# Gate rows through DRAM, an up projection with stationary tokens and transposes, and two modulation blocks per PSUM bank

## The chip, the cores and the metric

One core of a Trainium2 chip runs the whole program. The metric is the device time of one execution in microseconds (us), lower is better; 2327.01 us is the median of three runs of the kernel before.

## What is computed

One step of a transformer trunk with two layers, on 128 context tokens (`xp`) and 128 latent tokens (`xs`), width 2048, in fp32. Each layer makes six modulation vectors per stream from a conditioning vector (`w_ada`, 2048 x 12288), then an attention block and a squared-ReLU MLP of width 8192, both between RMS norms and with a gate on the residual. Cut to what matters here, for one of the two streams:

```python
sh_a, sc_a, gt_a, sh_m, sc_m, gt_m = split(silu(cvec) @ w_ada[l] + b_ada[l], 6)
h = rms_norm(x, g_pre_a) * (1 + sc_a) + sh_a
o = attention(h @ w_in[l]) @ w_out[l]
x = x + gt_a * rms_norm(o, g_post_a)
h = rms_norm(x, g_pre_m) * (1 + sc_m) + sh_m
x = x + gt_m * rms_norm(square(relu(h @ w_up[l])) @ w_down[l], g_post_m)
```

The two token streams pass through the same weights, each with its own modulation; the keys and values of the context tokens are outputs as well.

## The kernel before, in words

**Weights.** Every weight comes once from DRAM as a tile `raw` of 1 MB (128 x 2048), five in flight (`NRAW`), through SP's queue (`issue`, L994). Products are made from a high and a low half in fp32r: ACT copies half a tile to `wh` (L1011), DVE subtracts it to `wl` (L1012), and three matmuls (high x high, high x low, low x high) take the place of one. Three `wh`/`wl` pairs are in flight.

**Token-stationary groups.** The input, output and down projections use the class `Group` (L320): the tokens of stream s (`xh`, `xl`, 128 x 128) are stationary, 512 weight columns move, and a group of 1024 columns holds four accumulators, one PSUM bank each. In the last tile of a group each accumulator gets its last six matmuls together, and its `done` is called at once.

**Up projection.** The class `UpGroup` (L357) has the weights stationary (128 x 128) and the 256 tokens of both streams moving, so that the hidden units come out on the partitions, as the down projection needs them. A group is 512 hidden units in two banks; each bank gets a Relu, a square, a copy to the high half (ACT, L910, L911, L914) and a subtraction (DVE, L915). There are 16 groups in a layer; four of them and then a quarter of the down projection (2048 of 8192 rows) make one of the four rounds of the MLP.

**Modulation.** A block is 512 of a modulation vector's 2048 values, for both streams. Some blocks are made on PE (`ada_mm`, L139): 16 small matmuls from four raw tiles into one bank, a copy to `pt` (ACT, L150), four transposes, a reduction on DVE. The others are made on DVE (`dv_mul`, L195): `w_ada` transposed, multiplied by silu(c) broadcast to all partitions (`sB`), two passes (L201) for each of four tiles. The first two blocks come in halves of 256 columns. Lists of blocks are woven between the weight tiles by `weave`, and the generators in `fast`, `slow` and `dvq` are stepped once a half tile.

**Gates.** The gate of a block stays on the partitions (`gates`, L153) and is needed along the free axis. `gate_bc` (L277) transposes a broadcast column 128 x 128 four times on PE for each stream and each 512 columns: in the output projection a copy (L859) puts it in `rows`, ahead of the last tile of each half; at the end of the down projection DVE multiplies straight from PSUM (L934).

The code is recorded in this order, and a scheduler then sets the order on each engine from a model of its own; the section on the change shows places of it.

Of the kernel before, what the change touches and what calls it, by code (L numbers as in the profile page):

```python
# [67 lines left out]
def trunk(ctx: ExitStack, tc: tile.TileContext, I, O):  # L68
# [23 lines left out]
    sT = const.tile([P, KT, 32], F32, name="sT")  # L92
# [9 lines left out]
    st1 = const.tile([P, 8], F32, name="st1")  # L102
# [19 lines left out]
    def startup():  # L122
# [10 lines left out]
        for v in range(2):  # L133
            act.activation(sT[:, :, v], cT[:, v, :], AF.Silu)
# [4 lines left out]
    def ada_mm(l, sec, blk, kq, raw, half=None):  # L139

        w = 512 if half is None else 256
        if kq == 0:
            ada_live["ps"] = ps.tile([P, 512], F32, tag="ada", bufs=1, name="ada")
        pa = ada_live["ps"]
        for g in range(4):
            pe.matmul(pa[32 * g:32 * g + 32, 0:w], sT[:, 4 * kq + g, :], raw[:, g * w:(g + 1) * w],  # L146
                      start=(kq == 0), stop=(kq == 3), tile_position=(0, 32 * g))
        if kq == 3:
            pt = sb([P, 512], "pt")
            mark["pt"] = act.activation(pt[:, 0:w], pa[:, 0:w], AF.Copy)  # L150
            fast.append(ada_post(l, sec, blk, pt, 0 if half is None else 2 * half, w // P))

    gates = [const.tile([P, KT, 2], F32, name=f"gate{w}") for w in range(2)]  # L153
    made = set()

    def ada_post(l, sec, blk, pt, j0, nj):
# [5 lines left out]
        red = st1[:, 0:2 * nj].rearrange("p (j v) -> p j v", v=2)  # L162
        dve.tensor_reduce(red, m[:, 0:nj * P].rearrange("p (j g c) -> p j c g", g=4, c=32)[:, :, 0:2, :], AX.X,
                          ALU.add)
        if sec in (2, 5):
            gate_fin(l, sec, blk, red)
        else:
            mod_fin(l, sec, blk, red, j0, nj)
# [17 lines left out]
    sB = [const.tile([P, D], F32, name=f"sB{v}") for v in range(2)]  # L186
    dv_live = {}

    def load_sb():
        for v in range(2):  # L190
            nc.sync.dma_start(sB[v], I["crow"][v:v + 1, :].to_broadcast([P, D]))
        for v in range(2):
            act.activation(sB[v], sB[v], AF.Silu)

# [18 lines left out]
    def gate_fin(l, sec, blk, red):  # L213
# [3 lines left out]
        for v in range(2):  # L217
            o = gates[w][:, k0:k0 + 4, v]
            dve.tensor_tensor(o, red[:, :, v], baT[:, l, 16 * sec + k0:16 * sec + k0 + 4], ALU.add)
            dve.tensor_tensor(o, o, ngT[:, l, 2 * w + 1, k0:k0 + 4], ALU.mult)  # L220
        made.add((l, w, blk))

# [53 lines left out]

    def gate_bc(l, w, s, n):  # L277

        m = psm()
        assert (l, w, n) in made  # L280
        for j in range(4):
            tr(m[:, j * P:(j + 1) * P], gates[w][:, 4 * n + j, s:s + 1].to_broadcast([P, P]))
        return m
# [72 lines left out]

    class UpGroup:  # L357


        def __init__(self, done):  # L360
            self.done = done
            self.acc = None
            self.cnt = 0

        n = 1

# [19 lines left out]
        def left(self):  # L386
            return KT - self.cnt
# [753 lines left out]
```

## Time and profile before

| | |
|---|---|
| three runs | 2328.2, 2325.15, 2327.01 us; median 2327.01 |
| the profiled execution | 2328.18 us, its span 2326.2 us |
| PE busy | 2256.3 us, 97% of the span |
| DVE busy | 1596.9 us, 69% |
| ACT busy | 1091.7 us, 47% |
| DMA | 601.22 MB, 258 GB/s over the span |
| granted TensorE clock | 0.991 |

The span runs from the first to the last instruction of the program; the 2 us that remain lie around it. Busy times of engines overlap. The input and output projections of layer 0 take the time to about 480 us, its MLP to 1211 us; layer 1 follows, with its MLP from 1588 to 2313 us. PE stands for matmuls, and a matmul's row shows a modelled end, so the distance between two starts is the better measure of its cost in a dense stretch.

### The profile page before, as it was taken

To read this page: it belongs to the slowest core of one execution; us is meant where nothing else is said; L and a number is where in the kernel's file an instruction comes from. 1 tells how busy PE (TensorE), PEld (TensorE's weight loads), DVE (VectorE), ACT (ScalarE), POOL (GpSimd) and SP (SyncE) were. 2 spreads that over 40 slices of the span, in tenths; PEclk is the share of its full clock that TensorE was granted. 3 is DMA by queue.
4 is the path that set the end of the run, shared out by engine and by line. 5 is a ranking of instruction groups with operands and counts; after the bars stand their busy time and mean duration, and the time that the engine had idled before them with its cause. 6 is when DMAs were issued, how large, how long until landed. Compare 5 with 4: busy or idle time off the path is not lost.

```text
span 2326.2 us, 32947 instructions
## 1 busy us (share of the span) xinstructions
PE 2256.3 (97%) x13448; PEld 1905.2 (82%) x13448; DVE 1596.9 (69%) x1980; ACT 1091.7 (47%) x1508; POOL 24.6 (1%) x30
## 2 busy tenths in 40 slices
PE   6999999989999999999999999998999999999997
PEld 3567666679899889889877877877989989988986
DVE  2566745388988998998758787547566566565445
ACT  4334445365444445435446455546544444443543
POOL 0000000000000000000000000000000000000000
PEclk9999999999999999999999999999999999999999
DMA  8888787877877777787856666665566566666552
GB/s 336 302 337 338 285 314 292 345 275 283 312 296 293 279 289 292 275 304 287 344 195 258 245 248 223 227 235 201 216 235 224 204 225 219 215 219 216 182 181 91
DMA packets 92352, 601.22 MB, mean 258 GB/s; under 512 B 13736, under 2 KB 16040, under 8 KB 21288
## 3 DMA queue, kind: packets, MB, share of 16 engines
q1 hardware_dynamic: 91624, 598.64, 69.6%
q8 instruction: 105, 1.72, 0.3%
q10 hardware_dynamic: 576, 0.48, 0.1%
q14 instruction: 47, 0.39, 0.0%
HBM read 591.48 MB, written 7.60 MB: 258 GB/s over the span
## 4 chain that ended last, share of the span: by engine, by line
PE 84%; DVE 8%; DMA 4%; issue 2%; ACT 2%; POOL 1%; POOLq 0%; DVEq 0%; SPq 0%; ACTq 0%
PE acc L345 16%; PE acc L344 16%; PE acc L346 16%; PE acc L381 10%; PE acc L380 10%; PE acc L379 10%; PE ada L146 3%; DVE wl L1012 3%; PE m L120 2%; DMA raw<-w_adaT_in 2%; DVE raw L201 1%; POOL st L107 1%; PE m L467 1%; DVE stg L305 1%; ACT wh L1011 0%
## 5 line engine op out<-in xcount | busy, mean ns | idle before, releaser
L1011 ACT ACTIVATE wh<-raw 128x1024 fp32r<-128x1024 f32 x720 | 758.8, 1059 | 903.9 <-PE acc L346 527.8
L1012 DVE TENSOR_TENSOR wl<-raw,wh 128x1024 fp32r<-128x1024 f32 x720 | 874.2, 1222 | 429.6 <-ACT wh L1011 428.3
L379 PE MATMUL acc<-XT,wh 128*128 128x256 f32 x2048 | 580.1, 284 | 2.5 <-ACT XT L258 2.5
L381 PE MATMUL acc<-XT,wl 128*128 128x256 f32 x2048 | 580.7, 284 | 1.0 <-DVE wl L1012 1.0
L380 PE MATMUL acc<-XT,wh 128*128 128x256 f32 x2048 | 580.4, 284 | 0.3 <-DVE XT L259 0.3
L344 PE MATMUL acc<-wh,big 128*128 128x512 f32 x1280 | 501.9, 394 | 0.0
L345 PE MATMUL acc<-wl,big 128*128 128x512 f32 x1280 | 500.1, 391 | 1.7 <-DVE wl L1012 1.6
L346 PE MATMUL acc<-wh,big 128*128 128x512 f32 x1280 | 497.9, 390 | 0.0
L379 PEld LDWEIGHTS acc<-XT,wh 128*128 128x128 f32 x2048 | 393.5, 192 | 3.4 <-ACT XT L258 3.2
L381 PEld LDWEIGHTS acc<-XT,wl 128*128 128x128 f32 x2048 | 393.6, 192 | 2.2 <-DVE wl L1012 2.2
L380 PEld LDWEIGHTS acc<-XT,wh 128*128 128x128 f32 x2048 | 393.7, 192 | 1.1 <-DVE XT L259 0.8
L344 PEld LDWEIGHTS acc<-wh,big 128*128 128x128 f32 x1280 | 240.3, 188 | 55.9 <-issue 3.4
L345 PEld LDWEIGHTS acc<-wl,big 128*128 128x128 f32 x1280 | 240.6, 188 | 53.3 <-DVE wl L1012 4.4
L346 PEld LDWEIGHTS acc<-wh,big 128*128 128x128 f32 x1280 | 240.3, 188 | 49.9
L344 PE MATMUL acc<-wh,XT 128*128 128x512 f32 x576 | 229.1, 408 | 6.7 <-ACT wh L1011 4.7
L201 DVE SCALAR_TENSOR_TENSOR junk<-raw,sB 128x2048 fp8e5<-128x2048 f32 x92 | 210.4, 2286 | 33.4 <-DMA raw<-w_adaT_in 33.3
L345 PE MATMUL acc<-wl,XT 128*128 128x512 f32 x576 | 228.1, 396 | 2.4 <-DVE wl L1012 2.4
L346 PE MATMUL acc<-wh,XT 128*128 128x512 f32 x576 | 226.2, 393 | 0.0
L201 DVE SCALAR_TENSOR_TENSOR raw<-raw,sB 128x2048 f32<-128x2048 f32 x92 | 210.0, 2283 | 0.0
L344 PEld LDWEIGHTS acc<-wh,XT 128*128 128x128 f32 x576 | 108.6, 190 | 45.8 <-ACT wh L1011 11.2
L345 PEld LDWEIGHTS acc<-wl,XT 128*128 128x128 f32 x576 | 109.3, 190 | 30.3 <-DVE wl L1012 7.0
L346 PEld LDWEIGHTS acc<-wh,XT 128*128 128x128 f32 x576 | 108.9, 189 | 22.7
(127 smaller groups left out, 1183.5 us busy)
## 6 DMA issues: line engine op xcount, KB each, us to landing
raw<-w_up_in SPq DMA_DIRECT2D x128, 1024.0 KB, 4.9
raw<-w_down_in SPq DMA_DIRECT2D x128, 1024.0 KB, 5.0
raw<-w_adaT_in SPq DMA_DIRECT2D x92, 1024.0 KB, 4.8
raw<-w_ada_in SPq DMA_DIRECT2D x80, 1024.0 KB, 6.4
raw<-w_in_in SPq DMA_DIRECT2D x72, 1024.0 KB, 6.5
raw<-w_out_in SPq DMA_DIRECT2D x32, 1024.0 KB, 4.9
XT<-w_ada_in SPq DMA_DIRECT2D x12, 1024.0 KB, 7.5
raw<-w_ada_in SPq DMA_DIRECT2D x16, 512.0 KB, 5.5
```

Source lines behind the costliest of these rows:

```text
L107: pool.tensor_tensor(out, out, hf[:, 0:width], ALU.pow)
L120: pe.transpose(out, in_, ident)
L146: pe.matmul(pa[32 * g:32 * g + 32, 0:w], sT[:, 4 * kq + g, :], raw[:, g * w:(g + 1) * w], start=(kq == 0), stop=(kq == 3), tile_position=( ...
L201: p = dve.scalar_tensor_tensor(o, raw, 1.0, sB[v], ALU.mult, ALU.mult, accum_out=a[:, j, v:v + 1], saturate=None if v else False)
L344: pe.matmul(a, xh, wh[:, c], start=first, stop=False)
L345: pe.matmul(a, xh, wl[:, c], start=False, stop=False)
L346: pe.matmul(a, xl, wh[:, c], start=False, stop=last)
L379: pe.matmul(a, wh[:, c], xh, start=first, stop=False)
L380: pe.matmul(a, wh[:, c], xl, start=False, stop=False)
L381: pe.matmul(a, wl[:, c], xh, start=False, stop=last)
L1011: act.activation(wh, r, AF.Copy)
L1012: behind(dve.tensor_tensor(wl, r, wh.bitcast(F32), ALU.subtract), mark["res"])
```

## The change

Three parts. The up projection uses `Group` with 1024 columns: tokens stationary, 512 weight columns moving; each finished accumulator goes through a Relu to SBUF, four transposes on PE, and then square, copy and subtraction (`up_evict`), one accumulator later (`flush_up`). Two modulation blocks made on PE accumulate in one bank: the second block uses a window of `sT` shifted by two columns, so that its two streams land in columns 2 and 3, and copy, transposes and reduction are made once for both. And the gates of all 2048 columns are transposed once (`gate_rows`, 32 x 128), stored in DRAM, and read back as broadcast rows: into `rows` ahead of the output projection's third last tile of each half, and into `sB` for the MLP, behind the last product that reads silu(c) there; layer 1 reads silu(c) back from DRAM. The products of layer 0's MLP are spread over tiles 4 to 115 of the stage instead of 4 to 119.

```diff
-    sT = const.tile([P, KT, 32], F32, name="sT")
+    sT = const.tile([P, KT, 34], F32, name="sT")
...
-    st1 = const.tile([P, 8], F32, name="st1")
+    st1 = const.tile([P, 16], F32, name="st1")
     def rstd(out, ss, n, width):
...
-            act.activation(sT[:, :, v], cT[:, v, :], AF.Silu)
+            act.activation(sT[:, :, 2 + v], cT[:, v, :], AF.Silu)
...
-    def ada_mm(l, sec, blk, kq, raw, half=None):
+    def ada_mm(l, blks, t, kq, raw, half=None):
...
-        if kq == 0:
+        if (t, kq) == (0, 0):
...
+        end = t == len(blks) - 1 and kq == 3
...
-            pe.matmul(pa[32 * g:32 * g + 32, 0:w], sT[:, 4 * kq + g, :], raw[:, g * w:(g + 1) * w],
-                      start=(kq == 0), stop=(kq == 3), tile_position=(0, 32 * g))
-        if kq == 3:
+            pe.matmul(pa[32 * g:32 * g + 32, 0:w], sT[:, 4 * kq + g, 2 - 2 * t:34 - 2 * t], raw[:, g * w:(g + 1) * w],
+                      start=((t, kq) == (0, 0)), stop=end, tile_position=(0, 32 * g))
+        if end:
...
-            fast.append(ada_post(l, sec, blk, pt, 0 if half is None else 2 * half, w // P))
-    gates = [const.tile([P, KT, 2], F32, name=f"gate{w}") for w in range(2)]
+            fast.append(ada_post(l, blks, pt, 0 if half is None else 2 * half, w // P))
+    gates = [const.tile([P, 2, KT], F32, name=f"gate{w}") for w in range(2)]
...
-    def ada_post(l, sec, blk, pt, j0, nj):
+    gate_d = {}
+    def ada_post(l, blks, pt, j0, nj):
...
-        red = st1[:, 0:2 * nj].rearrange("p (j v) -> p j v", v=2)
-        dve.tensor_reduce(red, m[:, 0:nj * P].rearrange("p (j g c) -> p j c g", g=4, c=32)[:, :, 0:2, :], AX.X,
+        nv = 2 * len(blks)
+        red = st1[:, 0:nv * nj].rearrange("p (j v) -> p j v", v=nv)
+        dve.tensor_reduce(red, m[:, 0:nj * P].rearrange("p (j g c) -> p j c g", g=4, c=32)[:, :, 0:nv, :], AX.X,
...
-        if sec in (2, 5):
-            gate_fin(l, sec, blk, red)
-        else:
-            mod_fin(l, sec, blk, red, j0, nj)
+        for t, (sec, blk) in enumerate(blks):
+            r = red[:, :, 2 * t:2 * t + 2]
+            if sec in (2, 5):
+                gate_fin(l, sec, blk, r)
+            else:
+                mod_fin(l, sec, blk, r, j0, nj)
     def mod_fin(l, sec, blk, red, j0=0, nj=4):
...
+    sB_d = dp.tile([2, D], F32, name="silu")
...
     def load_sb():
...
+            nc.sync.dma_start(sB_d[v:v + 1, :], sB[v][0:1, :])
+    def reload_sb():
+        for v in range(2):
+            nc.sync.dma_start(sB[v], sB_d[v:v + 1, :].to_broadcast([P, D]))
     def dv_mul(l, sec, blk, j, raw, release):
...
-            o = gates[w][:, k0:k0 + 4, v]
+            o = gates[w][:, v, k0:k0 + 4]
...
+        if all((l, w, b) in made for b in range(4)):
+            fast.append(gate_rows(l, w))
+    def gate_rows(l, w):
+        yield
+        m = psm()
+        tr(m[0:2 * KT, 0:P], gates[w].rearrange("p v k -> p (v k)"))
+        yield
+        t = sb([2 * KT, P], "gr")
+        act.activation(t, m[0:2 * KT, 0:P], AF.Copy)
+        gate_d[l, w] = dp.tile([2, D], F32, tag="gd", bufs=2, name="gd")
+        nc.sync.dma_start(gate_d[l, w].rearrange("v (k p) -> (v k) p", p=P), t)
+    def load_gates(l, w, rows, c):
+        for v in range(2):
+            nc.sync.dma_start(rows[v][:, c], gate_d[l, w][v:v + 1, c].to_broadcast([P, c.stop - c.start]))
...
     def st2():
...
-    def gate_bc(l, w, s, n):
...
-        for j in range(4):
-            tr(m[:, j * P:(j + 1) * P], gates[w][:, 4 * n + j, s:s + 1].to_broadcast([P, P]))
-        return m
     def store_x():
...
         def left(self):
...
-    class UpGroup:
...
-            for f in range(4):
-                a = self.acc[f // 2][:, f % 2 * 256:f % 2 * 256 + 256]
-                c = slice(f * P, (f + 1) * P)
-                for i, (kt, wh, wl) in enumerate(steps):
-                    first = f % 2 == 0 and self.cnt + i == 0
-                    last = f % 2 == 1 and self.cnt + i == KT - 1
-                    xh, xl = XT[kt // 4][:, kt % 4, 0, :], XT[kt // 4][:, kt % 4, 1, :]
-                    pe.matmul(a, wh[:, c], xh, start=first, stop=False)
-                    pe.matmul(a, wh[:, c], xl, start=False, stop=False)
-                    pe.matmul(a, wl[:, c], xh, start=False, stop=last)
...
     def lhs_of(tiles, base=0):
         def f(kt, s, p):
...
-    fast, slow, dvq = [], [], []
+    fast, slow, dvq, pend = [], [], [], []
+    def flush_up():
+        while pend:
+            f, *a = pend.pop(0)
+            f(*a)
     def step_list(lst, n):
...
     def ada_items(l, blocks):
-        return [("ada", I["w_ada"][_pe_no(l, b), kq], (l, *b, kq)) for b in blocks for kq in range(4)]
+        o = len(blocks) % 2
+        sets = [blocks[:o]] * o + [blocks[i:i + 2] for i in range(o, len(blocks), 2)]
+        return [("ada", I["w_ada"][_pe_no(l, b), kq], (l, bs, t, kq))
+                for bs in sets for t, b in enumerate(bs) for kq in range(4)]
     def dv_items(l, blocks):
...
-            h0 = lambda h: [("ada", I["w_ada0"][sec, h, kq], (0, sec, 0, kq, h)) for sec in range(2) for kq in range(4)]
+            h0 = lambda h: [("ada", I["w_ada0"][sec, h, kq], (0, M_A[:2], sec, kq, h)) for sec in range(2) for kq in range(4)]
...
+            cG[0].insert(1, ("call", reload_sb))
...
-                for s in range(2):
-                    for n in range(2 * nh, 2 * nh + 2):
-                        act.activation(S["rows"][s][:, n * 512:(n + 1) * 512], gate_bc(l, 0, s, n), AF.Copy)
+                load_gates(l, 0, S["rows"], slice(1024 * nh, 1024 * nh + 1024))
...
         def wout_done(nh, S=S, l=l):
...
-            rest.insert(-1, ("call", wout_gates(nh)))
+            rest.insert(-3, ("call", wout_gates(nh)))
...
+        def up_evict(A, t, s):
+            m = psm()
+            for j in range(4):
+                tr(m[:, j * P:(j + 1) * P], t[:, j * P:(j + 1) * P])
+            u = sb([P, 512], "tmp", NTMP)
+            act.activation(u, m, AF.Square)
+            hi = A[:, :, 0, s * P:(s + 1) * P]
+            uv = u.rearrange("p (j q) -> p j q", j=4)
+            act.activation(hi, uv, AF.Copy)
+            dve.tensor_tensor(A[:, :, 1, s * P:(s + 1) * P], uv, hi.bitcast(F32), ALU.subtract)
         def up_done(g, M=M):
-            def f(i, a):
-                if i == 0:
-                    M["a"][g] = sb([P, 4, 2, 256], "big", 5, F32R)
-                A = M["a"][g]
-                t = sb([P, 512], "tmp", NTMP)
+            def f(s, n, a, _):
+                if s == 0:
+                    M["a"][2 * g + n] = sb([P, 4, 2, 256], "big", 5, F32R)
+                t = sb([P, 512], "qT", 2)
...
-                act.activation(t, t, AF.Square)
-                hi = A[:, 2 * i:2 * i + 2, 0, :]
-                tv = t.rearrange("p (f q) -> p f q", f=2)
-                act.activation(hi, tv, AF.Copy)
-                dve.tensor_tensor(A[:, 2 * i:2 * i + 2, 1, :], tv, hi.bitcast(F32), ALU.subtract)
+                flush_up()
+                pend.append((up_evict, M["a"][2 * g + n], t, s))
...
         def down_done(q, nh, M=M, l=l):
...
-                    m = gate_bc(l, 1, s, nt)
-                    dve.tensor_tensor(rw[:, c], rw[:, c], m, ALU.mult)
+                    dve.tensor_tensor(rw[:, c], rw[:, c], sB[s][:, c], ALU.mult)
...
-            load, use = ahead(ada_items(1, M_M[4:5]))
+            last = ada_items(1, G_A[3:] + M_M[4:5])
+            load, use = ahead(last[4:])
...
-            for g in range(4):
-                rest += tchunks(I["w_up"][l], 4 * (4 * q + g), 4, UpGroup(up_done(4 * q + g)), k4)
+            for g in range(2 * q, 2 * q + 2):
+                rest += tchunks(I["w_up"][l], 8 * g, 8, Group(2, KT, xl, up_done(g)), k2)
...
-            weave(rest[4:119], [], dv)
-            call(lambda: drain_dv())
+            weave(rest[4:115], [], dv)
+            call(lambda: (drain_dv(), drain_fast()))
+            items.append(rest[115])
+            call(lambda l=l: load_gates(l, 1, sB, slice(0, D)))
...
-            items.extend(rest[119:])
-            items.extend(ada_items(1, G_A[3:]))
+            items.extend(rest[116:])
+            items.extend(last[:4])
...
-            call(lambda: drain_dv())
-            items.extend(rest[100:])
+            call(lambda: (drain_dv(), drain_fast()))
+            items.append(rest[100])
+            call(lambda l=l: load_gates(l, 1, sB, slice(0, D)))
+            items.extend(rest[101:])
         def after_mlp(M=M, l=l, use=use):
...
-            l, sec, blk, kq, *half = it[2]
...
-            ada_mm(l, sec, blk, kq, r, *half)
+            ada_mm(*it[2][:4], r, *it[2][4:])
...
+                flush_up()
...
-    g["w_up"] = _f(np.concatenate([tiles(v["w_up"][:, :, o:o + 512], 4) for o in range(0, 8192, 512)], 1))
+    g["w_up"] = _f(np.concatenate([tiles(v["w_up"][:, :, o:o + 1024], 2) for o in range(0, 8192, 1024)], 1))
```

PE at the end of a group of the up projection in layer 1 (last of a round; `qT` holds the Relu's output, `m` the transposes). Before:

```order
L379 MATMUL acc_18885<-XT3_13305,wh_19026 128x256
L380 MATMUL acc_18885<-XT3_13305,wh_19026 128x256
L381 MATMUL acc_18885<-XT3_13305,wl_19027 128x256
L344 MATMUL acc_19129<-wh_19056,big_18355 128x512 [waits Activation_49]
L345 MATMUL acc_19129<-wl_19057,big_18355 128x512 [waits DVE_49]
L346 MATMUL acc_19129<-wh_19056,big_18355 128x512
```

The down projection follows at once. Now:

```order
L366 MATMUL acc_12198<-wl_12421,XT3_11745 128x512
L367 MATMUL acc_12198<-wh_12420,XT3_11745 128x512
L120 MATMUL m_12500<-cs_75,qT_12481 128x128 [waits Activation_49]
L120 MATMUL m_12500<-cs_75,qT_12481 128x128 x3
L365 MATMUL acc_12524<-wh_12438,big_12127 128x512
L366 MATMUL acc_12524<-wl_12439,big_12127 128x512 [waits DVE_49]
L367 MATMUL acc_12524<-wh_12438,big_12127 128x512
L365 MATMUL acc_12525<-wh_12438,big_12127 128x512
L120 MATMUL m_12509<-cs_75,qT_12498 128x128 [waits Activation_49]
L120 MATMUL m_12509<-cs_75,qT_12498 128x128 x3
L366 MATMUL acc_12525<-wl_12439,big_12127 128x512
```

Ahead of these rows the first two batches stand behind the second and the third accumulator's six matmuls; the fourth batch stands four matmuls into the next group.

ACT at the same place (Relu, then the passes of `up_evict`; L1020 is the split of a weight tile). Before, at the end of one group:

```order
L910 ACTIVATE tmp_18846<-acc_18639 128x512 [waits PE_49]
L911 ACTIVATE tmp_18846<-tmp_18846 128x512 [waits Activation_49]
L914 ACTIVATE big_18845<-tmp_18846 128x2x256 [waits Activation_49]
L1011 ACTIVATE wh_18815<-raw_18540 128x1024 [waits DVE_49,PE_49]
L910 ACTIVATE tmp_18875<-acc_18640 128x512 [waits PE_49]
L1011 ACTIVATE wh_18880<-raw_18574 128x1024 [waits DMAHW7_49,DVE_49]
```

Now:

```order
L918 ACTIVATE qT_12455<-acc_12195 128x512 [waits PE_49]
L918 ACTIVATE qT_12464<-acc_12196 128x512 [waits PE_49]
L907 ACTIVATE tmp_12471<-m_12466 128x512 [waits PE_49]
L910 ACTIVATE big_12454<-tmp_12471 128x4x128 [waits Activation_49]
L918 ACTIVATE qT_12481<-acc_12197 128x512 [waits PE_49]
L907 ACTIVATE tmp_12488<-m_12483 128x512 [waits PE_49]
L910 ACTIVATE big_12463<-tmp_12488 128x4x128 [waits Activation_49]
L1020 ACTIVATE wh_12442<-raw_12322 128x1024 [waits DVE_49,PE_49]
L918 ACTIVATE qT_12498<-acc_12198 128x512 [waits PE_49]
L907 ACTIVATE tmp_12505<-m_12500 128x512 [waits PE_49]
L1020 ACTIVATE wh_12520<-raw_12356 128x1024 [waits DMAHW7_49,DVE_49]
```

Four Relus and their passes stand within one group end, with a split ahead of the last Relu.

SP at the start of layer 1 (`xd` is the store of x, `silu` the rows in DRAM). Now:

```order
L1007 DMA raw_8871<-w_in_in 128x2048 [waits DMAHW5_49,DVE_49]
L204 DMA sB0_96<-silu_98 128x2048 [waits DVE_49]
L1007 DMA raw_8893<-w_adaT_in 128x2048 [waits DMAHW6_49,PE_49]
L1007 DMA raw_8958<-w_in_in 128x2048 [waits DMAHW7_49,PE_49]
L1007 DMA raw_8964<-w_in_in 128x2048 [waits DMAHW0_49,PE_49]
L1007 DMA raw_8970<-w_in_in 128x2048 [waits DMAHW2_49,DVE_49]
L1007 DMA raw_8976<-w_adaT_in 128x2048 [waits DMAHW1_49,PE_49]
L204 DMA sB1_97<-silu_98 128x2048 [waits DVE_49]
```

The two L204 rows are new; the weight tiles between and behind them stand in the order that they had.

## Rows read from the trace of the kernel before

**Rows 1.** The page: PE's busy time, and the chain's shares by engine.

```profile
PE 2256.3 (97%) x13448; PEld 1905.2 (82%) x13448; DVE 1596.9 (69%) x1980; ACT 1091.7 (47%) x1508; POOL 24.6 (1%) x30
...
PE 84%; DVE 8%; DMA 4%; issue 2%; ACT 2%; POOL 1%; POOLq 0%; DVEq 0%; SPq 0%; ACTq 0%
```

**Rows 2.** Windows: us, busy (instructions) by engine, clock, DMA; up quarters, layers 0, 1.

```profile
665.80:759.00 93.20, 92.83 (x771) 92.38 (x770) 82.20 (x83) 46.42 (x55) 0.00 (x0) 1.00 0.76 283
...
1772.00:1864.00 92.00, 92.00 (x769) 91.96 (x768) 53.43 (x51) 46.06 (x55) 0.00 (x0) 1.00 0.58 207
```

**Rows 3.** Timeline (start, length in us) of PE in the up projection, 52 starts apart.

```profile
519.74 0.28 PE L380 MATMUL acc<-XT,wh 128*128 128x256 f32 x1
...
525.98 0.28 PE L381 MATMUL acc<-XT,wl 128*128 128x256 f32 x1
```

**Rows 4.** Timeline of PE in the down projection, 20 starts apart.

```profile
599.76 0.39 PE L346 MATMUL acc<-wh,big 128*128 128x512 f32 x1
...
604.29 0.39 PE L345 MATMUL acc<-wl,big 128*128 128x512 f32 x1
```

**Rows 5.** Timeline of PE, layer 1's last down quarter: gate transposes behind every six matmuls.

```profile
2262.23 0.60 PE L120 MATMUL m<-cs,gate 128*128 128x128 f32 x4
...
2264.06 0.60 PE L120 MATMUL m<-cs,gate 128*128 128x128 f32 x4
...
2265.89 0.60 PE L120 MATMUL m<-cs,gate 128*128 128x128 f32 x4
```

**Rows 6.** Timeline: ACT's passes at a group end of layer 1; a matmul and its reader.

```profile
1861.54 0.60 ACT L910 ACTIVATE tmp<-acc 128x512 f32<-128x512 f32 x1 [1.94 <-PE acc L381]
...
1862.17 0.63 ACT L911 ACTIVATE tmp<-tmp 128x512 f32<-128x512 f32 x1
...
1862.83 0.63 ACT L914 ACTIVATE big<-tmp 128x512 fp32r<-128x512 f32 x1
...
1864.55 0.58 ACT L910 ACTIVATE tmp<-acc 128x512 f32<-128x512 f32 x1
...
1865.02 1.05 ACT L1011 ACTIVATE wh<-raw 128x1024 fp32r<-128x1024 f32 x1
...
1865.97 0.62 ACT L911 ACTIVATE tmp<-tmp 128x512 f32<-128x512 f32 x1
...
2263.82 0.40 PE L346 MATMUL acc<-wh,big 128*128 128x512 f32 x1
...
2264.26 0.69 DVE L928 TENSOR_TENSOR stg<-stg,acc 128x512 f32<-128x512 f32 x1 [0.28 <-PE acc L346]
```

**Rows 7.** Groups of the page (count; busy us, mean ns; idle before): a product's first pass.

```profile
L201 DVE SCALAR_TENSOR_TENSOR junk<-raw,sB 128x2048 fp8e5<-128x2048 f32 x92 | 210.4, 2286 | 33.4 <-DMA raw<-w_adaT_in 33.3
```

**Rows 8.** Timeline where layer 1 starts: gate multiply, weight issues, first product that reads sB.

```profile
1212.98 0.68 DVE L934 TENSOR_TENSOR stg<-stg,m 128x512 f32<-128x512 f32 x1
...
1213.19 1.62 SPq L998 DMA_DIRECT2D raw<-w_in_in  x3
...
1247.49 2.28 DVE L201 SCALAR_TENSOR_TENSOR junk<-raw,sB 128x2048 fp8e5<-128x2048 f32 x1
```

**Rows 9.** Window over layer 0's attention and its projections.

```profile
24.00:475.00 451.00, 433.14 (x2262) 294.37 (x2266) 248.93 (x449) 198.44 (x335) 9.53 (x9) 0.99 0.83 317
```

**Rows 10.** Timeline of PE: waits for copies of modulation blocks (idle before, what ended it).

```profile
63.76 0.66 PE L120 MATMUL m<-cs,pt 128*128 128x128 f32 x4 [0.72 <-ACT pt L150]
...
467.19 1.06 PE L146 MATMUL ada<-raw,sT 128*32 128x512 f32 x8 [2.34 <-ACT pt L150]
...
472.63 1.06 PE L146 MATMUL ada<-XT,sT 128*32 128x512 f32 x8 [1.08 <-ACT pt L150]
...
1223.05 0.66 PE L120 MATMUL m<-cs,pt 128*128 128x128 f32 x4 [2.18 <-ACT pt L150]
```

**Rows 11.** The chain that ended last, in order of time: two pieces between stages.

```profile
472.63 1.06 PE ada L146 x8
...
1221.00 2.74 DVE stg L305 x4
```

More of the change, by code (lines that the diff above doesn't have):

```diff
@@ L275, in st2 @@
         return sb([P, 8], "st2", 8)
-    def gate_bc(l, w, s, n):
-        m = psm()
-        assert (l, w, n) in made
-        for j in range(4):
-            tr(m[:, j * P:(j + 1) * P], gates[w][:, 4 * n + j, s:s + 1].to_broadcast([P, P]))
-        return m
     def store_x():
@@ L355, in left @@
             return self.segs[self.q + 1] - self.cnt
-    class UpGroup:
[L360 to L365, printed above, removed]
-        def run(self, steps):
-            if self.acc is None:
-                self.acc = [ps.tile([P, 512], F32, tag="acc", bufs=NACC, name="acc") for _ in range(2)]
-            end = self.cnt + len(steps) == KT
-            for f in range(4):
-                a = self.acc[f // 2][:, f % 2 * 256:f % 2 * 256 + 256]
-                c = slice(f * P, (f + 1) * P)
-                for i, (kt, wh, wl) in enumerate(steps):
-                    first = f % 2 == 0 and self.cnt + i == 0
-                    last = f % 2 == 1 and self.cnt + i == KT - 1
-                    xh, xl = XT[kt // 4][:, kt % 4, 0, :], XT[kt // 4][:, kt % 4, 1, :]
-                    pe.matmul(a, wh[:, c], xh, start=first, stop=False)
-                    pe.matmul(a, wh[:, c], xl, start=False, stop=False)
-                    pe.matmul(a, wl[:, c], xh, start=False, stop=last)
-                if end and f % 2:
-                    self.done(f // 2, self.acc[f // 2])
-            self.cnt += len(steps)
-        def left(self):
-            return KT - self.cnt
     def lhs_of(tiles, base=0):
```

## Prediction

> **What bounds the kernel now.** I read the page first: PE is busy 97% of the span and holds 84% of the chain that ended last [rows 1], so a term counts only if it shortens what PE does, or what PE waits for. Next came the windows by stage. In the MLP of layer 1 PE is never idle: a quarter of the up projection takes 92.0 us with DVE busy 53.4. In layer 0, where DVE also forms most modulation products, the same quarter takes 93.2 us with DVE busy 82.2 [rows 2]. So layer 1 follows PE to the tenth; layer 0 nearly does, with DVE close behind. The rest is the order of instructions, since the change alters what stands next to what.
>
> **Up projection, rate.** Before: 2048 matmuls on each of three lines, 6144 in all, 256 columns each. The two starts of [rows 3] are 52 matmuls apart: 6.24/52 = 0.1200 us. After: the class of the down projection does the work, 8 groups x 16 k-tiles x 2 x 2 x 3 = 1536 matmuls of 512 columns a layer, 3072 in all, and the starts of [rows 4] are 20 apart: 4.53/20 = 0.2265 us. 6144 x 0.1200 = 737.3 against 3072 x 0.2265 = 695.8: **-41.5 us**, all on PE's path.
>
> The Trainium skill speaks against this term: TensorE: Matmul & The Clock Gate, Back-to-back issue gap, gives columns/2.4 GHz plus 2.5 ns for a warm matmul, so two of 256 (218 ns) would cost nearly what one of 512 does (216 ns); by it this term would be an estimated -8 us and the sum below 2332.9. The trace does not agree (240 against 226.5), and the measurement decides.
>
> **Up projection, transposes.** Each finished 128x512 accumulator now needs four PE transposes: 16 groups x 4 = 64 batches. The row for exactly this is the last down quarter, where four gate transposes follow every six 512-column matmuls: three batches lie 1.83 us apart [rows 5]; 1.83 - 6 x 0.2265 = 0.471 a batch. 64 x 0.471 = **+30.1 us**. ACT still does three passes and DVE one for each 128x512, so nothing is added there.
>
> **The end of a group.** The four accumulators of a group finish six matmuls apart, so ACT gets twelve passes in a burst where it had three at a time. The order of PE and ACT shows the place: the fourth batch of transposes stands four matmuls into the next group and needs the fourth Relu, and on ACT one weight split (wh) stands ahead of that Relu. Count from the start of the last matmul of the first accumulator. PE reaches the batch at 3 x (1.36 + 0.471) + 0.227 + 0.91 = 6.6 us. A reader starts 0.44 after its matmul's start (2263.82 to 2264.26), ACT passes that depend on each other follow at 0.63 and 0.66, others at 0.47 (Relu) and 0.95 (split), and a Relu lasts 0.6 [rows 6]. Along ACT's order: Relus at 0.44 and 1.80, Square 2.28, copy 2.94, Relu 3.63, Square 4.11, copy 4.77, split 5.3, fourth Relu 6.24 to 6.83. PE waits some 0.3 us: 16 x 0.29 = **+4.6 us**. Bounds: zero if ACT is a little ahead; 16 x 0.77 = 12.3 if each pass takes its full length.
>
> **Layer 0's DVE.** The burst there also meets products of 2.28 us, two per tile [rows 7], and the 64 tiles must now be done by chunk 115 instead of 119 of the stage. Layer 0 is about 1.2 us a quarter slower than layer 1 today [rows 2], some 8 us over the stage; I add half of that again, **+4.0 us**. Below: 0. Above: a full pair, 4.6 us, at each of the 8 group ends.
>
> **Gates.** 128 transposes in 32 batches leave PE, 16 batches at dense places of the output projections, 16 at the end of the down projections: 32 x 0.471 = **-15.1 us**. The 16 ACT copies go too; ACT is not the path. What comes back on PE is four single transposes and their switches, 4 x 0.14 = +0.6. The rows now come by DMA, and what stands behind it on SP matters. (a) Output projection: the loads are called three chunks ahead, 16 us of PE, and the slots that they reuse are those of heads whose attention is over by then; were one late, the weight tiles behind it would be late by as much. (b) The MLP's row loads wait for the last product and the gate store, with about five weight tiles prefetched, some 25 us of cover. (c) The reload of the silu rows in layer 1 waits for the last use of sB as gates, and the w_in tiles stand behind it. Those were issued at 1213.2 and the gate multiply of the first half also ends near 1213.7; the first product that reads sB starts at 1247.5 [rows 8]. So each is hidden; 2.1 MB more per layer in a stage that moves 317 GB/s [rows 9] costs me **+1.0 us**, bounds 0 and the full 6.6.
>
> **Modulation blocks in pairs.** 23 blocks of four transposes become 12, four half-width ones become two. Of the 11 batches saved, three stand between stages (below); 8 x 0.471 = 3.8, and two half batches at 0.25. Also, PE waits for ACT's copy of the block: 0.72 at 63.76 [rows 10], four times alike in the first input projection. I drop two of those, and two more for the half-width blocks: 4 x 0.72 = 2.9. Sum **-7.1 us** (0.47 x 8 = -3.8 if the waits stay).
>
> **Between stages.** Before the first MLP, PE waits 2.34 and 1.08 for block copies [rows 10]; with the last block accumulating on top of its partner there is no copy to wait for. The chain that ended last runs through those very blocks at 472.63 [rows 11], so I take -3.0 (0 to -3.9). In the two later pauses, PE waits 2.18 at 1223.05 [rows 10] on a copy, but the chain runs through the residual on DVE at 1221.00 [rows 11]; I take one ACT pass, 0.6 each. **-4.2 us** together.
>
> **Sum.** -41.5 + 30.1 + 4.6 + 4.0 - 15.1 + 0.6 + 1.0 - 7.1 - 4.2 = **-27.6 us**. The profiled execution took 2328.2, which gives 2300.6; the median of the runs is 1.2 lower, so I forecast **2299.4 us**.
>
> **Rivals.** (A) *The fourth batch never waits and DVE absorbs the burst*: -27.6 - 8.6 = -36.2, 2290.8 us. For it: the idle share of DVE in layer 1. Against: the split ahead of the fourth Relu. (B) *ACT is the late one*: 0.77 a group end, 7.7 more, 2307.1 us. For it: the full lengths; against: the closer starts of [rows 6]. (C) *Transfers pace layer 0's attention*, so that its gate batches (3.8), its pairs (7.1) and its pause (3.0) return nothing and 2.1 MB cost 6.6: -27.6 + 13.9 + 5.6 = -8.1, 2318.9 us. For it: 0.83 of the DMA engines' time is taken there [rows 9]; against: PE's waits in that stage name ACT, not a transfer. (D) **Slower**: at each group end of layer 0 the weight difference wl that PE needs next stands behind a pair of products. Without any group-end cost in layer 0 the sum is -33.9, so this decides at 4.2 us per group end; at 4.6 + 0.3 it gives +5.2, 2332.2 us. For it: products and differences alternate on DVE, which has little slack [rows 2]. Against: PE has two splits in hand, 24 matmuls or 5.4 us. (E) *Width buys nothing*: if streaming columns set the pace, a 512-column matmul of the up projection costs two of the old ones, 0.240, the rate term is 0 and the sum +13.9, 2340.9 us. Against it stands the pitch of the same class of matmul in the down projection [rows 4]. The skill's rule above lies close to this case.
>
> **Chances.** My forecast 0.55; A 0.18; B 0.10; C 0.08; D 0.07; E 0.02. Some 0.2% (4.7 us) is what a measurement of this kernel can tell from no change. A, B, most of C and nearly all of the forecast are faster by more: 0.87; within it 0.05; slower 0.08. The range must reach past A, past B and to C: 2287 to 2320.
>
> **What would show it.** Right: in layer 1 an up quarter falls to about 87.0 + 8 x 0.471 + 2 x 0.3 = 91.4 from 92.0, the last down quarter, rid of its 8 batches, falls by 3.8; no gate transposes of 128x128; 52 pt transposes; PE idle of about 0.3 before the fourth qT batch of a group. Wrong: a pitch of the new matmuls other than 0.2265; a batch dearer than 0.5; PE waits on wl at the group ends of layer 0 of over 2 us; a wait of SP on the reload that reaches PE near 1230.

## The result, and the profile after

The changed kernel takes 2299.41 us, the median of four runs (2295.36 to 2303.17), against 2327.61 us for the kernel before in the same comparison: ratio 0.9871, 95% interval 0.9853 to 0.9888, 28.2 us less where 27.6 were forecast. The profiled execution took 2295.36 us with a span of 2293.3, the quickest of the four, so its stages add up to 32.9 us less than those of the profile before. Run again on another occasion the same kernel gave 2295.95 us, ratio 0.9856 (0.9839 to 0.9872), and a profiled span of 2300.2, 6.9 us more. By the two medians the gain is thus 28 to 32 us. That spread of some 7 us between executions is the limit to what single profiles tell, and an experiment on the changed kernel has to be set against both of its ratios, 0.9871 and 0.9856.

The page of the kernel after, its busy times, shares of the chain and the new passes:

```profile
PE 2223.2 (97%) x10460; PEld 1746.8 (76%) x10460; DVE 1592.6 (69%) x1967; ACT 1072.2 (47%) x1483; POOL 23.3 (1%) x30
...
PE 82%; DVE 7%; DMA 4%; ACT 3%; issue 2%; POOL 1%; SPq 0%; POOLq 0%; DVEq 0%; ACTq 0%
...
L918 ACT ACTIVATE qT<-acc 128x512 f32<-128x512 f32 x64 | 37.9, 594 | 18.9 <-PE acc L367 17.9
```

PE is still 97% busy, with 33 us less to do than in [rows 1]; the bound has not changed. L918 is the Relu of the new `up_evict` path, 64 of them as counted.

Windows over the MLP of layer 0 and of layer 1, and layer 0's attention, first of the kernel after and then of the kernel before (columns as in [rows 2]):

```profile
469.20:1190.90 721.70, 719.25 (x3224) 589.65 (x3225) 633.94 (x655) 337.66 (x398) 0.00 (x0) 1.00 0.80 292
1561.90:2280.90 719.00, 718.41 (x3227) 591.80 (x3225) 426.63 (x418) 338.43 (x399) 0.00 (x0) 1.00 0.58 205
25.00:452.40 427.40, 413.29 (x2125) 283.14 (x2125) 238.33 (x414) 181.35 (x296) 6.33 (x6) 0.99 0.85 326
```

```profile
481.50:1210.90 729.40, 726.40 (x4660) 661.96 (x4661) 634.02 (x655) 340.28 (x395) 0.00 (x0) 1.00 0.77 284
1587.70:2312.90 725.20, 725.13 (x4656) 663.95 (x4656) 427.21 (x418) 339.20 (x393) 0.00 (x0) 1.00 0.56 200
24.50:462.60 438.10, 424.15 (x2189) 291.82 (x2190) 240.20 (x424) 190.41 (x312) 7.76 (x6) 0.99 0.83 315
```

Each window runs from the first to the last projection matmul of its stage. Layer 0's MLP lost 7.7 us, layer 1's 6.2, layer 0's attention 10.7; the three pauses between stages lost 5.2, layer 1's attention 2.7, and what lies ahead of and behind the stages 0.4.

The new matmuls, on the timeline of PE in layer 1's up projection, 54 starts apart:

```profile
1797.84 0.39 PE L366 MATMUL acc<-wl,XT 128*128 128x512 f32 x1
...
1810.08 0.39 PE L366 MATMUL acc<-wl,XT 128*128 128x512 f32 x1
```

12.24/54 = 0.2267 us, as [rows 4] gave for the same class (0.2265). And one group end of layer 1, PE's batches of transposes and ACT's passes on the same timeline:

```profile
1831.61 0.60 PE L120 MATMUL m<-cs,qT 128*128 128x128 f32 x4
...
1833.43 0.60 PE L120 MATMUL m<-cs,qT 128*128 128x128 f32 x4
1833.63 0.60 ACT L918 ACTIVATE qT<-acc 128x512 f32<-128x512 f32 x1
...
1835.27 0.60 PE L120 MATMUL m<-cs,qT 128*128 128x128 f32 x4
1835.29 1.04 ACT L1020 ACTIVATE wh<-raw 128x1024 fp32r<-128x1024 f32 x1
1836.23 0.58 ACT L918 ACTIVATE qT<-acc 128x512 f32<-128x512 f32 x1
...
1836.87 0.42 PEld L120 LDWEIGHTS m<-cs,qT 128*128 128x128 f32 x4 [0.51 <-ACT qT L918]
1836.87 0.66 PE L120 MATMUL m<-cs,qT 128*128 128x128 f32 x4
```

The split L1020 stands ahead of the fourth Relu on ACT, and PE's fourth batch waits for that Relu, as the order had shown. Counted from the starts of the matmuls around each of the 64 batches, the first three of a group cost 0.447, 0.458 and 0.461 us in the mean, the fourth 0.744, 33.8 us in all.

### The profile page after: what moved, and what is told of

Same layout as the page of the kernel before. It is cut to its first block, busy times and chain, and to the rows that moved or that the text cites. A ratio compares the mean times of both kernels' runs of the same rounds, so it can differ in the third digit from the quotient of the medians.

```text
span 2293.3 us, 26818 instructions
## 1 busy us (share of the span) xinstructions
PE 2223.2 (97%) x10460; PEld 1746.8 (76%) x10460; DVE 1592.6 (69%) x1967; ACT 1072.2 (47%) x1483; POOL 23.3 (1%) x30
## 4 chain that ended last, share of the span: by engine, by line
PE 82%; DVE 7%; DMA 4%; ACT 3%; issue 2%; POOL 1%; SPq 0%; POOLq 0%; DVEq 0%; ACTq 0%
PE acc L366 25%; PE acc L367 25%; PE acc L365 25%; DVE wl L1021 3%; PE m L120 3%; PE ada L147 2%; DMA raw<-w_adaT_in 2%; ACT wh L1020 1%; ACT qT L918 1%; DMA raw<-w_in_in 1%; POOL st L107 1%; DMA raw<-w_ada_in 1%; DVE junk L212 1%; PE m L456 1%; DVE stg L326 0%
## 5 line engine op out<-in xcount | busy, mean ns | idle before, releaser
L1020 ACT ACTIVATE wh<-raw 128x1024 fp32r<-128x1024 f32 x720 | 759.2, 1060 | 961.1 <-PE acc L367 862.2
L365 PE MATMUL acc<-wh,XT 128*128 128x512 f32 x1600 | 629.0, 399 | 10.8 <-ACT XT L287 5.9
L366 PE MATMUL acc<-wl,XT 128*128 128x512 f32 x1600 | 629.5, 394 | 4.9 <-DVE wl L1021 4.6
L367 PE MATMUL acc<-wh,XT 128*128 128x512 f32 x1600 | 625.9, 392 | 0.0
L365 PEld LDWEIGHTS acc<-wh,XT 128*128 128x128 f32 x1600 | 301.3, 189 | 91.1 <-ACT wh L1020 14.1
L366 PEld LDWEIGHTS acc<-wl,XT 128*128 128x128 f32 x1600 | 301.9, 189 | 74.0 <-DVE wl L1021 13.4
L367 PEld LDWEIGHTS acc<-wh,XT 128*128 128x128 f32 x1600 | 301.7, 189 | 61.9
L212 DVE SCALAR_TENSOR_TENSOR junk<-raw,sB 128x2048 fp8e5<-128x2048 f32 x92 | 210.4, 2286 | 13.5 <-DMA raw<-w_adaT_in 13.0
L147 PE MATMUL ada<-raw,sT 128*32 128x512 f32 (+1 forms) x768 | 95.0, 574 | 15.2 <-DMA raw<-w_ada_in 15.1
L147 PEld LDWEIGHTS ada<-raw,sT 128*32 128x32 f32 x768 | 20.8, 110 | 60.1 <-issue 36.6
L911 DVE TENSOR_TENSOR big<-tmp,big 128x512 fp32r<-128x512 f32 x64 | 43.8, 687 | 30.1 <-ACT big L910 29.8
L775 DVE TENSOR_TENSOR stg<-stg,acc 128x512 f32<-128x512 f32 x64 | 42.8, 684 | 27.6 <-PE acc L367 27.4
L918 ACT ACTIVATE qT<-acc 128x512 f32<-128x512 f32 x64 | 37.9, 594 | 18.9 <-PE acc L367 17.9
L107 POOL TENSOR_TENSOR st<-st,hf 128x1 f32<-128x1 f32 (+2 forms) x26 | 23.1, 894 | 2263.7 <-DVE st L106 2068.9
```

What stands on the lines that cost most here:

```text
L107: pool.tensor_tensor(out, out, hf[:, 0:width], ALU.pow)
L147: pe.matmul(pa[32 * g:32 * g + 32, 0:w], sT[:, 4 * kq + g, 2 - 2 * t:34 - 2 * t], raw[:, g * w:(g + 1) * w], start=((t, kq) == (0, 0)), st ...
L212: p = dve.scalar_tensor_tensor(o, raw, 1.0, sB[v], ALU.mult, ALU.mult, accum_out=a[:, j, v:v + 1], saturate=None if v else False)
L365: pe.matmul(a, xh, wh[:, c], start=first, stop=False)
L366: pe.matmul(a, xh, wl[:, c], start=False, stop=False)
L367: pe.matmul(a, xl, wh[:, c], start=False, stop=last)
```

## Experiments

Ratios are to runs of the kernel before on the same chip.

**One part of the change at a time.** First the kernel before with the up projection alone:

```diff
-            for g in range(4):
-                rest += tchunks(I["w_up"][l], 4 * (4 * q + g), 4, UpGroup(up_done(4 * q + g)), k4)
+            for g in range(2 * q, 2 * q + 2):
+                rest += tchunks(I["w_up"][l], 8 * g, 8, Group(2, KT, xl, up_done(g)), k2)
...
+                flush_up()
```

> The kernel before with the new up projection alone; gates and modulation blocks as they were. Theory (the trace of after: no DVE cost in layer 0; first three batches 0.455 us, the fourth 0.75): -41.5 from the rate, +33.8 from the 64 batches, so -7.7 us against before, 2319.9 from 2327.6, ratio 0.9967. Rival (the terms as predicted, with 4.0 us of DVE in layer 0): -2.8 us, ratio 0.9988. Rival (the width of a matmul buys nothing): +34 us, ratio 1.0145.

Measured: 2319.48 against 2328.41 us, ratio 0.9957 (0.9945 to 0.9970), 8.9 us less by the medians. Both rivals lie outside the interval. The fourth batch costs 0.755 us here too, so the stall belongs to this part and to nothing else in the change.

The kernel before with the pairs of modulation blocks alone (`ada_mm`, `ada_post`, `ada_items`, the wider `sT` and `st1` of the diff):

```diff
+        sets = [blocks[:o]] * o + [blocks[i:i + 2] for i in range(o, len(blocks), 2)]
+        return [("ada", I["w_ada"][_pe_no(l, b), kq], (l, bs, t, kq))
+                for bs in sets for t, b in enumerate(bs) for kq in range(4)]
```

> The kernel before with the pairs of modulation blocks alone. Theory: the batches and copies saved (-7.1) and the shorter pauses between stages (-4.2) are all the pairs' doing: -11.3 us, ratio 0.9951, with the pause ahead of layer 1's MLP down from 17.7 us to about 15. Rival: the later pauses belong to the gates or to DVE, and the pairs give the batches alone: -5 us, ratio 0.9979.

Measured: 2316.29 us, ratio 0.9938 (0.9926 to 0.9951), 12.1 us less. The size is the theory's; the place is not. The pause ahead of layer 1's MLP fell from 17.7 to 16.8 us and not to 15, the other two by 1.0 and 0.9, and layer 0's attention carries 8.4 us.

The kernel before with the gates alone (`gate_rows`, `load_gates`, `reload_sb`, and the end of the products at tile 115):

```diff
-                    m = gate_bc(l, 1, s, nt)
-                    dve.tensor_tensor(rw[:, c], rw[:, c], m, ALU.mult)
+                    dve.tensor_tensor(rw[:, c], rw[:, c], sB[s][:, c], ALU.mult)
```

> The kernel before with the gate rows through DRAM alone. Theory: 32 batches of transposes at 0.471 us leave PE's path, four single transposes come back, nothing waits for the loads: -14.5 us, ratio 0.9938; the last quarter of the down projection in each layer falls by 3.8 us. Rival: a load or the reload of the silu rows is late and PE waits for it near the start of layer 1 or in an output projection: -8 us or less, ratio above 0.9965.

Measured: 2324.01 us, ratio 0.9981 (0.9972 to 0.9990), 4.4 us less. The rival's number, but not its place: the output projection of layer 1 fell from 102.7 to 98.9 us and the last down quarters by 3.0 and 3.3, near the 3.8 forecast for each. The loss lies in layer 0's first up quarter, 107.1 us where it had 96.0. Windows over that quarter, of the run with the gates on SP and of the kernel before:

```profile
480.10:587.20 107.10, 98.84 (x792) 97.92 (x793) 87.86 (x103) 53.63 (x76) 0.00 (x0) 0.95 0.66 238
```

```profile
481.50:577.50 96.00, 95.54 (x792) 94.90 (x793) 87.32 (x102) 53.73 (x76) 0.00 (x0) 1.00 0.76 271
```

The same matmuls, but PE stood idle for 8.3 of the 107.1 us, and the granted clock fell to 0.95 in the mean. PE has two long waits, by its timeline in the run with the gates:

```profile
557.85 0.39 PE L396 MATMUL acc<-XT,wh 128*128 128x256 f32 x1 [2.96 <-ACT wh L1030]
...
563.31 0.58 PE L398 MATMUL acc<-XT,wl 128*128 128x256 f32 x1 [4.72 <-DVE wl L1031]
```

Ahead of that DVE, by its timeline in the same run, begins no product between 531.5 and 557.5 us, and then makes two passes in a row, behind the evictions (L931, the passes that empty a finished accumulator):

```profile
531.47 2.29 DVE L208 SCALAR_TENSOR_TENSOR raw<-raw,sB 128x2048 f32<-128x2048 f32 x1
...
547.27 1.23 DVE L1031 TENSOR_TENSOR wl<-raw,wh 128x1024 fp32r<-128x1024 f32 x1 [1.60 <-ACT wh L1030]
554.01 0.69 DVE L931 TENSOR_TENSOR big<-tmp,big 128x512 fp32r<-128x512 f32 x1 [5.51 <-ACT big L930]
556.88 0.69 DVE L931 TENSOR_TENSOR big<-tmp,big 128x512 fp32r<-128x512 f32 x1 [2.18 <-ACT big L930]
557.49 2.28 DVE L208 SCALAR_TENSOR_TENSOR junk<-raw,sB 128x2048 fp8e5<-128x2048 f32 x1
559.82 2.29 DVE L208 SCALAR_TENSOR_TENSOR raw<-raw,sB 128x2048 f32<-128x2048 f32 x1
562.03 3.49 DVE L1031 TENSOR_TENSOR wl<-raw,wh 128x1024 fp32r<-128x1024 f32 x3
```

In the kernel before, products and differences alternate here, by DVE's timeline:

```profile
548.53 2.28 DVE L201 SCALAR_TENSOR_TENSOR raw<-raw,sB 128x2048 f32<-128x2048 f32 x1
...
550.74 1.22 DVE L1012 TENSOR_TENSOR wl<-raw,wh 128x1024 fp32r<-128x1024 f32 x1
551.88 2.28 DVE L201 SCALAR_TENSOR_TENSOR junk<-raw,sB 128x2048 fp8e5<-128x2048 f32 x1
```

ACT's order differs too, and the first of the two waits, for wh, is on it. In the run with the gates ACT makes no split from 547.2 to 556.8 us, where three follow each other behind both evictions; in the kernel before, splits start at 548.86, 553.90 and 555.34, among the evictions. So the gates would be worth what was forecast and the order took it back; to tell that from a cost of the transfers themselves, the two small stores of the silu rows (8 KB each) went to ACT's queue, which brings the old order of products back and moves the same bytes:

```diff
-            nc.sync.dma_start(sB_d[v:v + 1, :], sB[v][0:1, :])
+            nc.scalar.dma_start(sB_d[v:v + 1, :], sB[v][0:1, :])
```

> The kernel before with the gate rows alone, as in the run of the gates on SP, but the two small stores of the silu rows are issued from ACT's queue; this changes the order in which the scheduler puts products on DVE in the first up quarter back to what it was. Theory (the gates are worth what was forecast, and the earlier run lost 11 us to that order): -14.5 us against before, ratio 0.9938, the first up quarter of layer 0 at 96 us and not 107. Rival (the loads or stores themselves hold PE up): ratio 0.998 as in the earlier run.

Measured: 2314.34 against 2329.73 us, ratio 0.9931 (0.9917 to 0.9946), 15.4 us less; the quarter takes 97.3 us, 9.8 less than with the stores on SP, and the waits of PE in it (us in total, times, longest) are

```profile
PE acc L396 <- ACT XT L283: 2.2, 1, 2.2
PE acc L397 <- DVE XT L284: 0.3, 1, 0.3
PE acc L398 <- DVE wl L1031: 0.2, 1, 0.2
```

DVE makes its products among the differences again, by its timeline in this run:

```profile
550.64 2.28 DVE L208 SCALAR_TENSOR_TENSOR raw<-raw,sB 128x2048 f32<-128x2048 f32 x1
...
552.85 1.22 DVE L1031 TENSOR_TENSOR wl<-raw,wh 128x1024 fp32r<-128x1024 f32 x1
553.99 2.28 DVE L208 SCALAR_TENSOR_TENSOR junk<-raw,sB 128x2048 fp8e5<-128x2048 f32 x1
```

No wait of PE in this quarter names a transfer, though the loads and the reload add some 10.5 MB to the program (611.77 MB against 601.22). That the stores on SP make the scheduler choose the other order is shown by the pair of runs; why its model does so was not looked into.

Do the parts add up? The medians of the three (gates with the second order) give 8.9 + 12.1 + 15.4 = 36.4 us, their profiled spans 4.8 + 11.9 + 10.7 = 27.4; the whole change gave, on its two occasions, 28.2 and 32.4 by its medians, 32.9 and 26.0 by its profiled spans. Each part's interval is 3 us to either side, so an overlap of a few microseconds between them can neither be shown nor excluded.

**The stall at the group end.** The changed kernel, with the fourth batch put behind the next half tile:

```diff
-                flush_up()
+                if not whole:
+                    flush_up()
                 step_list(fast, 1)
```

> The changed kernel, with the fourth batch of transposes of each up group put 12 matmuls into the next group instead of 4. Theory: the fourth batch waits only because its Relu stands behind a weight split on ACT; moved, it costs 0.455 like the others: 16 x 0.29 = -4.7 us against after, 2294.7, ratio to before 0.9858. Rival: the wait moves on, since the squares and copies of the fourth accumulator then stand ahead of weight splits that PE needs: no change, ratio 0.9879.

Measured: 2293.54 us, ratio 0.9848 (0.9835 to 0.9862). The theory's 0.9858 lies in the interval, the rival's 0.9879 outside; but the changed kernel's own second ratio, 0.9856, lies inside as well, so the time alone does not decide between them. The trace does. The timeline of PE at a group end of layer 1 shows the third and the fourth batch:

```profile
1791.14 0.60 PE L120 MATMUL m<-cs,qT 128*128 128x128 f32 x4
...
1794.34 0.60 PE L120 MATMUL m<-cs,qT 128*128 128x128 f32 x4
```

3.20 - 12 x 0.2267 = 0.48: no wait is left, and over the 16 groups the fourth batch costs 0.466 in the mean. Layer 1's MLP fell by 2.7 us, 8 x 0.28 = 2.2 of it by this count. In layer 0 nothing was won (722.2 us after 721.7): by its timeline PE waited 3.3 us there for weight differences, in six places. The changed kernel has 1.3 us of these waits in its first profile and 3.2 in its second, where its layer 0 takes 722.8 us, so they differ by some 2 us between executions of one kernel.

**The width of a matmul.** The changed kernel, with every matmul of the up projection in two halves:

```diff
+                            for h in range(0, 512, self.width):
+                                e = h + self.width
+                                pe.matmul(a[:, h:e], x0, w0[:, n * 512 + h:n * 512 + e],
+                                          start=st and h == 0, stop=sp_ and e == 512)
```

> The changed kernel, with each 512-column matmul of the up projection issued as two of 256 columns on the same stationary tokens. Theory (the rate term is the width of a matmul): 3072 matmuls at 0.2265 us become 6144 at 0.1200, +41 us against after, 2341, ratio to before 1.005. Rival (the old projection was slower for another reason, its stationary weights or its four short accumulators, and 256 columns cost half of 512): no change, ratio 0.987. The Trainium skill, TensorE: Matmul & The Clock Gate, Back-to-back issue gap, would give +8 us, ratio 0.991.

Measured: 2343.21 us, ratio 1.0064 (1.0048 to 1.0081). On PE's timeline

```profile
1790.32 0.64 PE L369 MATMUL acc<-wh,XT 128*128 128x256 f32 x4
1790.80 0.40 PE L369 MATMUL acc<-wl,XT 128*128 128x256 f32 x2
...
1798.95 0.64 PE L369 MATMUL acc<-wh,XT 128*128 128x256 f32 x4
```

72 matmuls start in 8.63 us, 0.1199 each, though the tokens are stationary now: it is the width that costs, not what is stationary. The second up quarter of layer 1 takes 94.9 us where after has 89.9, and eight times 5.0 is 40 of the 44 to 47 us that the run is slower than the changed kernel on its two occasions. In layer 0's MLP PE waits 5.9 us for weight differences and 2.6 for a weight split, where after has 1.3 us of such waits; this was not followed up.

**DVE's load in layer 0.** The changed kernel, products on fewer tiles; the load of the gate rows behind them moves forward with them:

```diff
-            weave(rest[4:115], [], dv)
+            weave(rest[4:100], [], dv)
```

> The changed kernel, with the products of layer 0's MLP on tiles 4 to 100 of the stage instead of 4 to 115. Theory (DVE had room left at 115 and no more than that, so my +4.0 us did not come but the bound is near): without the products DVE is taken for 0.49 of the stage (352 of 722 us), the products are 283 us, so 588 of 626 us up to tile 115 (94%) and 547 of 541 us up to tile 100 (101%): PE is held up for 6 us or more, above 2305, ratio over 0.990. Rival (DVE has slack to spare and only the order of products makes PE wait): within 2 us of after, ratio 0.987 to 0.988.

Measured: 2294.16 us, ratio 0.9851 (0.9835 to 0.9866). My expectation failed. The rival's 0.987 to 0.988 was counted from the changed kernel's first ratio; the measured one agrees with its second, 0.9856. The stretch from 472 to 1000 us, by windows of this run and then of the kernel after:

```profile
472.00:1000.00 528.00, 526.81 (x2365) 432.13 (x2364) 520.97 (x539) 249.21 (x289) 0.00 (x0) 1.00 0.85 310
```

```profile
472.00:1000.00 528.00, 526.25 (x2359) 430.96 (x2359) 490.99 (x508) 248.39 (x288) 0.00 (x0) 1.00 0.81 295
```

DVE was busy for 521 of 528 us and PE lost nothing: its waits for weight differences there were 0.8 us in both, by the waits of PE in the run with the dense products:

```profile
PE acc L366 <- DVE wl L1021: 0.8, 2, 0.5
```

So the load by itself cost PE nothing here; what an order can cost, the run with the gates shows.

**These edits together.** The changed kernel with the fourth batch held back and the two stores on ACT's queue:

> The changed kernel with the fourth batch held back by 12 matmuls, and the two stores of the silu rows on ACT's queue. The run with the fourth batch alone gained 2.7 us in layer 1's MLP and none in layer 0's, where PE waited some 3 us for weight differences. Theory (order of the products on DVE): with the other order those waits shrink, 1 to 3 us less than with the fourth batch alone, some 2291.5, ratio 0.984. Rival (DVE's load sets them): no less than 2293, ratio 0.985.

Measured: 2290.93 us, ratio 0.9841 (0.9821 to 0.9860): the theory's figure, but the interval holds the rival's 0.985 too, and the 0.9848 of the run with the fourth batch alone. Layer 0's MLP takes 718.6 us in this profile, and PE waits 1.7 us in it for weight differences, between the 1.3 and 3.2 of the changed kernel's two profiles. That the stores on ACT's queue gain anything here is not shown. With the denser products as well:

> The changed kernel with all three edits: fourth batch held back by 12 matmuls, silu rows stored from ACT's queue, products of layer 0's MLP on tiles 4 to 100. Theory (DVE's load costs nothing up to 98.7% of a stretch, only the order of its work makes PE wait): the fourth batch is worth 4.5 us and the waits for weight differences in layer 0, 1.7 us of PE with the products up to tile 115, shrink to 1 or less: 1 to 2 us under the version without the denser products, some 2290 where before is 2328, ratio 0.9835. Rival (with the fourth batch moved, denser products collide with the group ends): slower than that version, ratio over 0.986.

Measured: 2290.94 us, ratio 0.9838 (0.9823 to 0.9853); the rival is excluded, a gain over the version before it is not to be seen. Beside it, on the same chip:

> The changed kernel once more, unchanged, on the chip of the run beside it, so that the two are compared with the same runs of the kernel before. Theory and rival alike: ratio 0.9871, inside 0.985 to 0.989.

Measured: 2295.95 us, ratio 0.9856 (0.9839 to 0.9872). Both versions are quicker than before by 37 to 39 us. Against the changed kernel beside it the second won 5 us by the medians; the intervals of the ratios overlap, but each of its four executions (2289.78 to 2292.00 us) lies under each of the changed kernel's four (2293.17 to 2302.28).

## Why the prediction was right, step by step

- **Rate, -41.5**: right. 6144 x 0.1200 - 3072 x 0.2267 = 40.9, and the halves gave it back. The sign that I had named, an up quarter of layer 1 at 91.4 us, counted all eight batches; the quarter takes 89.9 (1745.1 to 1835.0), as its last two batches stand behind its last matmul, in the down quarter. The Trainium skill (TensorE: Matmul & The Clock Gate, Back-to-back issue gap) would put two matmuls of 256 columns at 218 ns beside 216 for one of 512, by a rule that the section gives for a matmul in isolation. Here two of 256 columns cost 240 with either operand stationary and one of 512 costs 227 with the tokens stationary, the only case measured, so its 8 us were too small, and the choice of the trace's rows was the right one.
- **Transposes, +30.1, and the group end, +4.6**: 34.7 together, 33.8 measured. A batch is 0.455 and not 0.471, the stall 0.29 as forecast, at the place that the order of PE and ACT showed.
- **Layer 0's DVE, +4.0**: wrong, none of it came. I put layer 0's lag behind layer 1 at 8 us, from one quarter, and added half of it; over the whole MLP the lag was 4.2 us (729.4 - 725.2), and after the change it is 2.7 (721.7 - 719.0; 3.3 in the second profile). The step took DVE's busy share for a price. The dense run shows that 98.7% can cost nothing; the gates alone on SP, that nearly the same work in another order (87.9 us of DVE in the quarter where before has 87.3) goes with a loss of 11 us. Rival D had the right object (differences behind a pair of products), but not in the changed kernel: it came with the gates alone, once, behind the evictions of one group end (4.72 us where D had priced 4.9).
- **Gates, -13.5 with what came back**: 15.4 by the medians, measured alone with the better order, 10.7 by the profiled spans. Layer 1's output projection gave 3.8 us and the last down quarters 3.0 and 3.3, for batches priced at 3.8 each. Layer 0's output projection, where transfers are dense [rows 9], gave only 0.8 (157.7 to 156.9; 2.1 in the run with the stores on SP): there the term was too large in its place. PE's waits in that stretch name DVE and ACT in both kernels and no transfer, so why it gave so little stays open. The 2.1 MB that the term charges for each layer are the rows of the output projection alone; those of the MLP are as many again, and the reload is 2.1 MB more.
- **Pairs, -7.1 - 4.2**: 11.3 against 12.1, but distributed otherwise: the attention of layer 0 gave 8.4 where 7.1 was forecast, the three pauses 2.8 where it was 4.2. The term of 3.0 for the first pause was mis-sized; alone, the pairs gave 1.0 there.
- **Pauses after the change**: the one ahead of layer 1's MLP shrank by 2.9 where I had 0.6. The pairs alone gave 0.9, the gates 0.5, and the up projection 1.2, a gain that I had not listed: with the tokens stationary, its first matmuls need one stream only. On PE's timeline of the kernel before the first up matmul stands behind three batches of the input's transposes and a wait for XT, in that of the run with the up projection alone behind two:

```profile
1582.18 0.60 PE L120 MATMUL m<-cs,big 128*128 128x128 f32 x4
1585.07 2.34 PE L120 MATMUL m<-cs,big 128*128 128x128 f32 x8 [2.30 <-ACT big L242]
1587.74 0.80 PE L379 MATMUL acc<-XT,wh 128*128 128x256 f32 x2 [0.33 <-ACT XT L258]
```

```profile
1580.63 1.06 PE L120 MATMUL m<-cs,big 128*128 128x128 f32 x4
1583.85 1.11 PE L120 MATMUL m<-cs,big 128*128 128x128 f32 x4 [2.16 <-ACT big L242]
1584.61 0.78 PE L344 MATMUL acc<-wh,XT 128*128 128x512 f32 x1
```

The total is right to the microsecond partly by luck: executions of one kernel differ by more than any of these errors, the median of the changed kernel moved by 3.5 us from one occasion to the other, and the 4.0 us of DVE that did not come stand against 2.8 that the gates, by the profiled spans, did not give. Rival A's forecast, 2290.8, lies 5 to 9 us under the two medians: DVE did absorb the burst, but the stall that A denied is there. B's extra 0.48 at each group end did not come, C's transfers can have taken no more than 3 us from layer 0's gates, and E is excluded by the halves.

## What to carry to other kernels

Where one engine is never idle, price an edit by start-to-start distances of the same instruction in the same neighbourhood; the rate, the transposes, the stall, the gates and the pairs came out within 3 us that way. Write down ACT's order at the end of a group: one weight split ahead of a Relu cost 0.29 us sixteen times, and moving the transposes by one half tile removed it. Do not charge a busy share: DVE at 98.7% of a stretch cost PE nothing, and an amount of DVE work that cost little in one order went with 11 us in another, where long passes stood ahead of those that PE needed. After any edit to a queue, look at that order anew.

## What had not been expected of the hardware

PE can start again slowly after a pause. Ahead of layer 1's MLP, by windows of the kernel after:

```profile
1554.00:1562.00 8.00, 2.42 (x20) 1.73 (x13) 7.01 (x21) 4.53 (x12) 1.48 (x3) 0.80 1.01 424
1562.00:1566.00 4.00, 4.00 (x15) 3.22 (x14) 1.39 (x5) 3.03 (x8) 0.00 (x0) 0.55 0.14 57
1566.00:1580.00 14.00, 14.00 (x72) 11.37 (x71) 12.06 (x24) 12.45 (x24) 0.00 (x0) 1.00 0.28 82
```

After 8 us in which PE was busy for 2.42, the granted clock is 0.55, near the lower of its two levels (1.2 of 2.4 GHz), for the next 4 us, and 512-column matmuls start 0.43 us apart in it (1562.46, 1562.89, 1563.32) where they take 0.2267 later. That pause thus cost an estimated 2 us beyond its own length (4 us at 0.55). The change did not bring this: in the kernel before the clock is 0.50 from 1588 to 1592 us, at the same place. Not every pause does it: ahead of layer 0's MLP, where the matmuls of modulation blocks kept PE busy for 11.0 of 16 us (453 to 469 us of the kernel after), the clock stayed at 1.00. The 11 us that the gates alone lost hold a part of this kind, some 3 us by PE's busy time for the same matmuls (98.8 us against 95.5): the clock was 0.83 from 480 to 490 us, at the quarter's start, and 0.82 from 548 to 566.
